# One encoder kernel: expert weights in 8 KB pieces, router weights in two steps, and another order of work at the last tile

## The chip, the cores and the metric

The kernel runs on one core of one Trainium2 chip. The metric is the device time of one launch in microseconds (us); the span of the profile, from the first to the last instruction, is some 2 us shorter. The core's engines run side by side, each with its own queue of instructions: TensorE (PE; its weight loads are a row of their own, PEld), VectorE (DVE), ScalarE (ACT), GpSimd (POOL) and SyncE (SP), which here only issues transfers. Engines wait for one another on semaphores.

## What is computed

Two encoder layers on 1024 tokens of width 1024, all in float32. Layer 0 mixes tokens by neighbourhood attention, layer 1 by a chunked two-way mLSTM scan, both beside attention to a memory. After each mixer stand an output projection, a layer norm, a router and a mixture of 16 experts:

```python
x = layer_norm(ALPHA * x + mixed @ w_out[i], ln_g[i, 0], ln_b[i, 0])
x = layer_norm(ALPHA * x + moe(x, router_w, router_b, exp_w_gate[i], exp_w_up[i], exp_w_down[i]),
               ln_g[i, 1], ln_b[i, 1])
# in moe: two experts of one group per token, and for each expert on its rows
hb = silu(xb @ w_gate[e]) * (xb @ w_up[e])
return hb @ w_down[e]
```

`w_gate` and `w_up` are 1024 x 512, `w_down` is 512 x 1024, for each of 16 experts and both layers.

## The kernel before

**Products.** A float32 product is made of three `fp32r` matmuls: both operands are split into a high part (a cast on ScalarE, `w_hi`) and the remainder (a subtraction on VectorE, `w_lo`), and `mm3` (L105 to L107) adds high x high, high x low and low x high. In the trace's names the moving operand comes first, the stationary one second: `dense<-w_hi,yh` moves 512 columns of weights past 128 loaded columns of `yh`.

**Weights** come through a `WeightStream`: `load` issues transfers on SyncE's queue into raw buffers, `split` takes the next one and splits it (L77 on ScalarE, L78 on VectorE or on an engine that is passed), `pieces` does it in halves (L92, L93) that the caller places between other work, `next` hands over a split piece. A piece of expert weights is 1 MB: 4 blocks of 128 rows x 512 columns. Row `k*128 + p` of the matrix lies on partition `p`, so a partition's 8 KB come as four runs of 2 KB.

**Tail of a layer** (`out_proj`, L1843). Eight tiles of 128 tokens: `products` of the mixer's output with `w_out` in two halves of 512 columns, `sums` (the residual, and the norm's statistics), `turn` (the transposes of the sums, L1485), `logits` (L1491), `route` (a chain of small VectorE steps to L1559, begun by `begin` and run by `choose` with other work put between its steps), `ranks` (two matmuls that count tokens ahead of each one for its expert, L1573), `entries`, and `scatter` (token lists written to memory by GpSimd). A table `mid` puts such steps behind the k-th group of matmuls in a tile's first products; the order in which the code is written sets the rest, since each engine runs its instructions in the order of the program. Behind the last tile, expert 0's tokens are found from `first_sums` and `first_list` without the list in memory, its rows are gathered (`x`, 128 rows; `xb`, 64 rows), transposed (L2039 and L2089) and multiplied by the four pieces of its gate and up weights (`chunk(0)` to `chunk(3)`). `route_order` (from L1654) sorts the experts by their counts; the order sets which weights SyncE loads next. SyncE is held until `xb` has landed (`hold`).

**Experts** (`moe`). The experts run in the order of their counts; a wide one (up to 192 rows, 8 of them) and a narrow one (128 rows) in turn. For each: gather its rows (GpSimd), transpose them (L2170, and L2176 for the last 64), gate and up products into `dense` banks of PSUM (4), then, one expert later, transpose the hidden rows (L2255, L2262) and multiply by the two down pieces into `rlg` banks (2): per 512 output columns 12 matmuls for 128 rows (`pa`) and then, for a wide expert, 8 for its last 64 (`pb`, L2298, L2299). `evac` (L2289) scales a bank into `ya` on ScalarE; GpSimd adds the rows to the result in memory. `ahead` keeps up to three pieces split in advance; `flush` runs the evictions that are due.

**Between the layers**, `moe_norm` reads the eight tiles of the result (`z`), normalises them and hands them to layer 1's input products (`xp`, L831: transposes of normalised rows; L812, L817: splits of the weight pieces). A planner, `Plan`, sets the order from each step's engine, cost and due time. The weight stream there has two raw buffers, so the third piece can be loaded once the first is split.

**Router weights** (`router_weights`, L1420) are made once, in layer 0's attention: products and sums over rows (L1439, L1440), a matmul with ones (L1444), and what follows from it.

## Time and profile before

| | us |
|---|---|
| three runs, median (lowest to highest) | 2055.79 (2053.3 to 2058.6) |
| the profiled execution | 2056.02, span 2054.0 |
| TensorE busy | 1863.0 (91%) |
| VectorE busy | 1401.3 (68%) |
| ScalarE busy | 1080.4 (53%) |
| GpSimd busy | 457.1 (22%) |
| layer 0's tail | about 470 to 610 |
| experts of layer 0 | about 610 to 998 |
| layer 0 to layer 1, first matmul of layer 1's input | 1032.69 |
| layer 1's tail | about 1463 to 1617 |
| experts of layer 1 | about 1617 to 2010 |

A row of a timeline has the start, the duration, the engine, the line of the kernel, the operation, what it writes and reads, its shape, how many were put together (x4), and in brackets how long the engine was idle before it and what ended that. A row of the waits has the waiting engine, tile and line, what it waited for, and then the total in us, how often, and the longest. TensorE's matmuls overlap, so the distance from one start to the next tells the pace, not the duration.

### The profile page before, as it was taken

What the parts mean: (1) busy time and instruction counts of PE and PEld (TensorE: products, weight loads), DVE (VectorE), ACT (ScalarE), POOL (GpSimd) and SP (SyncE); (2) the same over time, 40 slices, a digit from 0 to 9 for tenths busy, and PEclk for the clock granted to TensorE, in tenths of its full rate; (3) what the DMA queues carried; (4) which work ended last, traced back from release to release, by engine and by line L of the source; (5) the groups of instructions that cost most, each with busy time, mean ns of one, the idle gap of its engine ahead of it and who ended that gap; (6) DMA issues with size and microseconds to landing.
All of it is one profiled execution on the core that took longest, in us unless ns stands there. A gap on an engine that the chain in (4) does not pass through costs nothing. (4 is left out here: it accounts for less than half of the span.)

```text
span 2054.0 us, 27927 instructions
## 1 busy us (share of the span) xinstructions
PE 1863.0 (91%) x9860; PEld 1552.1 (76%) x9860; DVE 1401.3 (68%) x2717; ACT 1080.4 (53%) x1772; POOL 457.1 (22%) x386
## 2 busy tenths in 40 slices
PE   7999999998979999999599899998798799999991
PEld 6788888877757877777398778887687587777771
DVE  5466656677767877777576554269878687777775
ACT  4465555662236666666454555444422465666663
POOL 1132222201221222222210000065422121222211
PEclk9999999999979999999799999999899899999996
DMA  5452321135538899999632222111664789999995
GB/s 186 118 134 61 68 56 39 53 121 169 189 130 293 286 297 306 311 309 305 196 128 70 63 82 75 62 32 49 212 207 150 230 267 291 297 309 306 298 286 185
DMA packets 252978, 371.19 MB, mean 181 GB/s; under 512 B 47820, under 2 KB 120868, under 8 KB 252836
## 3 DMA queue, kind: packets, MB, share of 16 engines
q1 hardware_dynamic: 237460, 320.00, 47.5%
q0 software_dynamic: 15376, 49.38, 9.5%
q8 instruction: 79, 1.29, 0.3%
q14 instruction: 63, 0.52, 0.1%
HBM read 300.43 MB, written 65.76 MB: 178 GB/s over the span
## 5 line engine op out<-in xcount | busy, mean ns | idle before, releaser
L78 DVE TENSOR_TENSOR w_lo<-w_raw,w_hi 128x2048 fp32r<-128x2048 f32 (+1 forms) x222 | 470.4, 2126 | 191.9 <-ACT w_hi L77 188.7
L77 ACT CAST w_hi<-w_raw 128x2048 fp32r<-128x2048 f32 (+1 forms) x224 | 396.9, 1780 | 62.9 <-DMA w_raw<-in_exp_w_gate_dram 47.2
L105 PE MATMUL dense<-xT_h,w_hi 128*128 128x512 f32 (+1 forms) x544 | 226.3, 416 | 0.9 <-ACT xT_h L192 0.9
L107 PE MATMUL dense<-xT_h,w_lo 128*128 128x512 f32 (+1 forms) x544 | 208.4, 383 | 1.7 <-DVE w_lo L78 1.7
L106 PE MATMUL dense<-xT_l,w_hi 128*128 128x512 f32 (+1 forms) x544 | 208.1, 383 | 1.0 <-DVE xT_l L193 1.0
L105 PE MATMUL dense<-w_hi,xah 128*128 128x512 f32 x480 | 195.9, 408 | 0.0
L107 PE MATMUL dense<-w_hi,xal 128*128 128x512 f32 x480 | 188.3, 392 | 0.0
L106 PE MATMUL dense<-w_lo,xah 128*128 128x512 f32 x480 | 187.9, 391 | 0.0
L2291 POOL DMA_INDIRECT accd<-ya,la x30 | 80.2, 2675 | 431.1 <-ACT ya L2289 419.6
L105 PE MATMUL dense<-w_hi,yh 128*128 128x512 f32 x288 | 127.6, 443 | 10.7 <-ACT yh L1868 10.6
L106 PE MATMUL dense<-w_lo,yh 128*128 128x512 f32 x288 | 119.9, 416 | 7.6 <-DVE w_lo L93 7.6
L342 ACT ACTIVATE att_p<-att_p,att_st 128x352 f32<-128x352 f32 (+1 forms) x96 | 57.9, 604 | 128.4 <-DVE att_st L340 126.2
L584 POOL TENSOR_TENSOR bias<-bias_raw,masks 128x352 f32<-128x352 f32 (+1 forms) x96 | 85.2, 893 | 163.6 <-DVE att_st L350 145.9
L107 PEld LDWEIGHTS dense<-xT_h,w_lo 128*128 128x128 f32 x544 | 103.6, 191 | 23.2 <-DVE w_lo L78 2.6
L107 PE MATMUL dense<-w_hi,yl 128*128 128x512 f32 x288 | 120.1, 417 | 0.2 <-DVE yl L1801 0.2
L351 DVE TENSOR_SCALAR att_p<-att_p,att_st 128x256 f32<-128x256 f32 (+2 forms) x160 | 112.4, 702 | 5.7
L106 PEld LDWEIGHTS dense<-xT_l,w_hi 128*128 128x128 f32 x544 | 104.6, 192 | 8.3 <-DVE xT_l L193 1.4
L105 PEld LDWEIGHTS dense<-xT_h,w_hi 128*128 128x128 f32 x544 | 104.4, 192 | 8.2 <-ACT xT_h L192 1.0
L105 PE MATMUL rlg<-w_hi,hah 128*128 128x512 f32 x256 | 103.9, 406 | 2.7 <-ACT hah L192 2.7
L107 PEld LDWEIGHTS dense<-w_hi,xal 128*128 128x128 f32 x480 | 90.1, 188 | 20.2
L107 PE MATMUL rlg<-w_hi,hal 128*128 128x512 f32 x256 | 101.4, 396 | 3.5 <-DVE hal L193 3.5
L2215 PE MATMUL dense<-w_hi,xbc 128*128 128x512 f32 x256 | 100.8, 394 | 3.8 <-DVE xbc L193 3.8
(448 smaller groups left out, 4308.9 us busy)
## 6 DMA issues: line engine op xcount, KB each, us to landing
w_raw<-in_exp_w_gate_dram SPq DMA_DIRECT2D x64, 1024.0 KB
w_raw<-in_exp_w_up_dram SPq DMA_DIRECT2D x64, 1024.0 KB
w_raw<-in_exp_w_down_dram SPq DMA_DIRECT2D x64, 1024.0 KB
w_raw<-in_na_w_in_dram SPq DMA_DIRECT2D x20, 512.0 KB
w_raw<-in_w_out_dram SPq DMA_DIRECT2D x8, 1024.0 KB
x1d<-z SPq DMA_DIRECT2D x16, 512.0 KB
accd<-za SPq DMA_DIRECT2D x16, 512.0 KB
z<-accd SPq DMA_DIRECT2D x16, 512.0 KB
```

Source lines behind the costliest of these rows:

```text
L77: self.nc.scalar.copy(h[:, :n], t[:, :n])
L78: (eng or self.nc.vector).tensor_tensor(l[:, :n], t[:, :n], h[:, :n].bitcast(F), op=OP.subtract)
L105: nc.tensor.matmul(out, lhsT=a[0], rhs=b[0], start=first, stop=False)
L106: nc.tensor.matmul(out, lhsT=a[0], rhs=b[1], start=False, stop=False)
L107: nc.tensor.matmul(out, lhsT=a[1], rhs=b[0], start=False, stop=last)
L342: nc.scalar.activation(self.p, self.p, AF.Exp, bias=st[:, 0:1], scale=-1.0, accum_out=st[:, 1:2])
L351: nc.vector.tensor_scalar(self.p, self.p, st[:, 2:3], None, op0=OP.mult)
L584: nc.gpsimd.tensor_tensor(b[:, :nr], rev[:, w0:w0 + nr, u0:u0 + 32], nb.masks[:, half * 3 + kind].rearrange("p (a b) -> p a b", b=32)[:, :nr],
L2215: nc.tensor.matmul(pb, lhsT=c[:, kk], rhs=w[0][:, k], start=kk == 0, stop=False)
L2291: nc.gpsimd.indirect_dma_start(out=accd[layer], out_offset=bass.IndirectOffsetOnAxis(ap=la[:, 0:1], axis=0), in_=ya, in_offset=None, compu ...
```

## The change

The parts, in the order of the program:

1. `router_weights` is a generator: its first part runs behind head pair 2, the matmul with ones and the rest behind head pair 3.
2. Layer 1's tail no longer splits a piece on GpSimd at the end of the scan.
3. In a tile, `ranks(t - 2)` stands behind group 6 of the first products, not group 1; in the last tile `ranks(5)` is part of the step behind group 3.
4. Behind the last tile: expert 0's rows are transposed within that tile's second products; the transposes of the last sums and `ranks(6)` go into `chunk(0)`; `chunk(1)` and most of `chunk(2)` come before `ranks(7)`; the counts are summed before the list of expert 0's last rows, and `route_order` comes before the last tile's entries and scatters. A sixth piece is loaded earlier.
5. Expert weights are laid out with row `p*8 + k` (gate, up) or `p*4 + k` (down) on partition `p`, so that a piece is one run of 8 KB per partition; a down piece holds two k for all 1024 columns. To match, the transposes of token and hidden rows take every 8th or every 4th column (`every`).
6. The down products of both column halves run side by side in two `rlg` banks, and those of a wide expert's last 64 rows go to two `dense` banks.
7. Between the layers SyncE issues the four weight pieces and the two norm rows before the loads of `z`.

```diff
                 if i == 2:
-                    router_weights(nb.pool)
+                    router = router_weights(nb.pool)
+                    next(router)
                 if i == 3:
+                    next(router)
                     layer1_consts()
...
             tl.ws.load(3)
-            tl.ws.split(nc.gpsimd)
             tl.advance()
...
-                mid = {1: [lambda: ranks(t - 2)], 2: [lambda: turn(t - 1, 0)], 4: [lambda: turn(t - 1, 1)],
-                       7: [lambda: logits(t - 1)]}
+                mid = {2: [lambda: turn(t - 1, 0)], 4: [lambda: turn(t - 1, 1)], 7: [lambda: logits(t - 1)]}
...
                     def filled():
+                        ranks(5)
                         p = count_sums(n)
...
+                else:
+                    mid[6] = [lambda: ranks(t - 2)]
...
-            products(7, 1, {1: [lambda: first_sums(chosen, 1, rows[1], True, False)], 6: [lambda: turn(7, 0)]})
+            def turn_x(q):
+                p = bank("rtr", 2)
+                for k in range(4):
+                    nc.tensor.transpose(p[:, k * 128:(k + 1) * 128], every(x, 8, 4 * q + k), ident)
...
+            products(7, 1, {1: [lambda: first_sums(chosen, 1, rows[1], True, False)], 2: [lambda: turn(7, 0)],
+                            5: [lambda: turn_x(0)], 6: [lambda: turn_x(1)]})
             store(6)
             sums(7, 1)
...
-            turn(7, 1)
             ws.load(ws.raw_bufs)
...
             fill = norm(7)
-            chunk(0)
+            chunk(0, {0: [lambda: ranks(6)], 1: [lambda: turn(7, 1)]})
             logits(7)
-            ranks(6)
             run(ws.pieces())
-            ws.load(2, nc.scalar)
-            run(fill[:2])
+            more = entries(6)
+            run(more[:1])
             begin(7)
-            run(fill[2:])
+            run(fill)
             store(7)
-            more = ws.pieces()
-            choose(7, entries(6) + [lambda: chosen.extend(first_select(sel, [6]))] + more)
+            ws.load(ws.raw_bufs)
+            more += [lambda: chosen.extend(first_select(sel, [6]))] + ws.pieces()
+            choose(7, more)
+            n = counts(rpool)
             scatter(6, 0)
             scatter(6, 1)
             chunk(1)
-            ranks(7)
+            chunk(2, {2: [lambda: ranks(7)]})
+            p = count_sums(n)
             fill = entries(7)
...
+            route_order(rpool, p)
+            run(ws.pieces())
+            ws.load(1)
             run(fill)
             scatter(7, 0)
             scatter(7, 1)
-            chunk(2)
-            route_order(rpool)
-            run(ws.pieces())
-            ws.load(1)
             chunk(3)
...
-                return v.rearrange("o (k p) c -> p (o k) c", p=128)[:, k0:k0 + nk, c0:c0 + ncol]
+                return v.rearrange("o (p k) c -> p (o k) c", p=128)[:, k0:k0 + nk]
...
-            ws.add(chunk(wd, i, 0, 4, 0, 512), (4, 512))
-            ws.add(chunk(wd, i, 0, 4, 512, 512), (4, 512))
+            ws.add(chunk(wd, i, 0, 2), (2, 1024))
+            ws.add(chunk(wd, i, 2, 2), (2, 1024))
...
+    def every(x, n, k):
+
+        return x.rearrange("t (p k) -> t k p", k=n)[:, k]
...
-                        nc.tensor.transpose(p[:, k * 128:(k + 1) * 128], xa[:, (4 * q + k) * 128:(4 * q + k + 1) * 128], ident)
+                        nc.tensor.transpose(p[:, k * 128:(k + 1) * 128], every(xa, 8, 4 * q + k), ident)
...
-                for n in range(2):
+                pa = [bank("rlg", 2), bank("rlg", 2)]
+                for c in range(2):
                     w = ws.next()
                     ws2.append(w)
-                    pa = bank("rlg", 2)
-                    for k in range(4):
-                        mm3(nc, pa, [th[:, k], tl[:, k]], [w[0][:, k], w[1][:, k]], k == 0, k == 3)
-                    if n:
-                        flush()
+                    for k in range(2):
+                        for n in range(2):
+                            mm3(nc, pa[n], [th[:, 2 * c + k], tl[:, 2 * c + k]], [x[:, k, n * 512:n * 512 + 512] for x in w],
+                                c + k == 0, c == 1 and k == 1)
                     ahead()
                     flush()
...
-                for n in range(2 if hb is not None else 0):
-                    w = ws2[n]
-                    pb = bank("rlg", 2)
...
+                pb = [bank("dense", 4), bank("dense", 4)]
+                for c in range(2):
+                    w = ws2[c]
+                    for k in range(2):
+                        for n in range(2):
+                            for m in range(2):
+                                nc.tensor.matmul(pb[n], lhsT=tc_[:, 2 * c + k], rhs=w[m][:, k, n * 512:n * 512 + 512],
+                                                 start=c + k + m == 0, stop=c == 1 and k + m == 2)
...
-        add_load(0)
+
+        for f in extra[:2]:
+            f()
         add_row("ln_g")
-        add_load(1)
         add_row("ln_b")
-        add_load(2)
-        for t in range(3, nbuf):
-            if extra:
-                extra.pop(0)()
+        for f in extra[2:]:
+            f()
+        sums_there = plan.op([], ("d", 0.0, lambda: None), lag=0.0 if rows else 9.0)
+        for t in range(nbuf):
             add_load(t)
```

**TensorE behind the last products, layer 0's tail, before.** `L1485` and `L2039` are transposes (of the sums, and of expert 0's rows), the `dense` rows from `yh` are products.

```order
L107 MATMUL dense<-w_hi,yl 128x512
L2039 MATMUL rtr<-ident,z 128x128 x8
L1485 MATMUL rtr<-ident,z 128x128 x4
L105 MATMUL dense<-w_hi,yh 128x512
L106 MATMUL dense<-w_lo,yh 128x512
L107 MATMUL dense<-w_hi,yl 128x512
```

**The same place now**, first within the last products (`L2041` are the transposes of expert 0's rows):

```order
L2041 MATMUL rtr<-ident,z 128x128 x4
L105 MATMUL dense<-w_hi,yh 128x512
L106 MATMUL dense<-w_lo,yh 128x512
L107 MATMUL dense<-w_hi,yl 128x512
L2041 MATMUL rtr<-ident,z 128x128 x4
L105 MATMUL dense<-w_hi,yh 128x512
```

and then where `chunk(0)` has begun (`L1576`, `L1577` are the ranks, `L1488` the transposes of the sums):

```order
L1576 LDWEIGHTS tri
L1576 MATMUL rlg<-rt,tri 128x16
L1577 LDWEIGHTS onesb
L1577 MATMUL rlg<-rt,onesb 128x16
L105 MATMUL dense<-w_hi,yh 128x512
L106 MATMUL dense<-w_lo,yh 128x512
L107 MATMUL dense<-w_hi,yl 128x512
L1488 MATMUL rtr<-ident,z 128x128 x4
```

The eight transposes of expert 0's rows moved from behind the products into them, and those of the last sums from ahead of the first chunk into it; `ranks(6)` came in from behind the logits.

**TensorE in expert 0's down projection, before** (the last group of `pa` and the first rows of `pb`):

```order
L106 MATMUL rlg<-w_lo,hah 128x512
L107 MATMUL rlg<-w_hi,hal 128x512
L2170 MATMUL rtr<-ident,xa 128x128 x4
L2298 MATMUL rlg<-w_hi,hbc 128x512
L2299 MATMUL rlg<-w_lo,hbc 128x512
```

**Now:**

```order
L106 MATMUL rlg<-w_lo,hah 128x512
L107 MATMUL rlg<-w_hi,hal 128x512
L2183 MATMUL rtr<-ident,xa 128x128 x4
L2315 MATMUL dense<-w_hi,hbc 128x512
L2315 MATMUL dense<-w_lo,hbc 128x512
```

The products of the last 64 rows moved from `rlg` to `dense`; the products of `pa` alternate between two `rlg` banks, which the rows don't tell.

**SyncE's queue between the layers, before:**

```order
L2407 DMA z<-accd_73 128x1024
L243 DMA ln_g<-in_ln_g_dram 128x1024
L2407 DMA z<-accd_73 128x1024
L243 DMA ln_b<-in_ln_b_dram 128x1024
L2407 DMA z<-accd_73 128x1024
L58 DMA w_raw<-in_ml_w_in_dram 128x8x128
L2407 DMA z<-accd_73 128x1024
L58 DMA w_raw<-in_ml_w_in_dram 128x8x128
L2407 DMA z<-accd_73 128x1024
L2407 DMA z<-accd_73 128x1024
L58 DMA w_raw<-in_ml_w_in_dram 128x8x128
```

**Now:**

```order
L58 DMA w_raw<-in_ml_w_in_dram 128x8x128 x2
L243 DMA ln_g<-in_ln_g_dram 128x1024
L243 DMA ln_b<-in_ln_b_dram 128x1024
L58 DMA w_raw<-in_ml_w_in_dram 128x8x128 x2
L2424 DMA z<-accd_73 128x1024
```

All four weight pieces and both rows now stand ahead of the first `z` load; before, that load stood ahead of all of them and the pieces between the loads.

More of the change, by code (lines that the diff above doesn't have):

```diff
@@ L1442, in router_weights @@
         nc.gpsimd.memset(one, 1.0)
+        yield
         p = bank("att_t", 2)
@@ L2031, in out_proj, with chunk @@
             choose(6, fill)
-            products(7, 1, {1: [lambda: first_sums(chosen, 1, rows[1], True, False)], 6: [lambda: turn(7, 0)]})
+            xh, xl = [epool.tile([128, 8, 128], R, name=n, tag=n, bufs=2) for n in ("yh", "yl")]
+            def turn_x(q):
+                p = bank("rtr", 2)
+                for k in range(4):
+                    nc.tensor.transpose(p[:, k * 128:(k + 1) * 128], every(x, 8, 4 * q + k), ident)
+                p = p.rearrange("p (k t) -> p k t", k=4)
+                split_from_psum(xh[:, 4 * q:4 * q + 4], xl[:, 4 * q:4 * q + 4], p)
+            products(7, 1, {1: [lambda: first_sums(chosen, 1, rows[1], True, False)], 2: [lambda: turn(7, 0)],
+                            5: [lambda: turn_x(0)], 6: [lambda: turn_x(1)]})
             store(6)
             sums(7, 1)
-            xh, xl = [epool.tile([128, 8, 128], R, name=n, tag=n, bufs=2) for n in ("yh", "yl")]
-            for q in range(2):
-                p = bank("rtr", 2)
-                for k in range(4):
-                    nc.tensor.transpose(p[:, k * 128:(k + 1) * 128], x[:, (4 * q + k) * 128:(4 * q + k + 1) * 128], ident)
-                p = p.rearrange("p (k t) -> p k t", k=4)
-                split_from_psum(xh[:, 4 * q:4 * q + 4], xl[:, 4 * q:4 * q + 4], p)
-            turn(7, 1)
             ws.load(ws.raw_bufs)
             e.w, e.p = [], []
-            def chunk(j):
+            def chunk(j, after={}):
                 if j % 2 == 0:
@@ L2088, in out_proj @@
             for k in range(8):
-                nc.tensor.transpose(p[:, k * 64:(k + 1) * 64], xb[:, k * 128:(k + 1) * 128], ident[:64, :64])
+                nc.tensor.transpose(p[:, k * 64:(k + 1) * 64], every(xb, 8, k), ident[:64, :64])
             split_from_psum(e.c[:, :, 0:64], e.c[:, :, 64:128], p.rearrange("p (k t) -> p k t", k=8))
@@ L2175, in rest @@
                     for k in range(8):
-                        nc.tensor.transpose(p[:, k * 64:(k + 1) * 64], xb[:, k * 128:(k + 1) * 128], ident[:64, :64])
+                        nc.tensor.transpose(p[:, k * 64:(k + 1) * 64], every(xb, 8, k), ident[:64, :64])
                     split_from_psum(c[:, :, 0:64], c[:, :, 64:128], p.rearrange("p (k t) -> p k t", k=8))
@@ L2254, in full @@
                     for k in range(4):
-                        nc.tensor.transpose(p[:, k * 128:(k + 1) * 128], ha[:, k * 128:(k + 1) * 128], ident)
+                        nc.tensor.transpose(p[:, k * 128:(k + 1) * 128], every(ha, 4, k), ident)
                     split_from_psum(th, tl, p.rearrange("p (k t) -> p k t", k=4))
@@ L2261, in rest @@
                     for k in range(4):
-                        nc.tensor.transpose(p[:, k * 64:(k + 1) * 64], hb[:, k * 128:(k + 1) * 128], ident[:64, :64])
+                        nc.tensor.transpose(p[:, k * 64:(k + 1) * 64], every(hb, 4, k), ident[:64, :64])
                     split_from_psum(tc_[:, :, 0:64], tc_[:, :, 64:128], p[:, :256].rearrange("p (k t) -> p k t", k=4))
@@ L2286, in down, with evac @@
                         fill.pop(0)()
[L2288 to L2299 removed]
+                def evac(n):
+                    nc.scalar.mul(ya[:, n * 512:n * 512 + 512], pa[n], la[:, 1:2].bitcast(F))
+                    if n == 1:
+                        nc.gpsimd.indirect_dma_start(out=accd[layer], out_offset=bass.IndirectOffsetOnAxis(ap=la[:, 0:1], axis=0),
+                                                     in_=ya, in_offset=None, compute_op=OP.add)
+                late.extend([lambda: evac(0), lambda: evac(1)])
+                if hb is None:
+                    return
+                pb = [bank("dense", 4), bank("dense", 4)]
[6 more added lines that the diff above has]
+                                                 start=c + k + m == 0, stop=c == 1 and k + m == 2)
                     flush()
@@ L2411, in add_load @@
         def add_load(t):
-            loads.append(plan.op(ends[t - nbuf] if t >= nbuf else [], ("s", 1.5, lambda: load(t)), lag=2.0))
+            loads.append(plan.op(ends[t - nbuf] if t >= nbuf else [sums_there], ("s", 1.5, lambda: load(t)), lag=2.0))
         def add_row(key):
```

42 lines of the change are left out of this document (16 added, 26 removed).

## The prediction

> **What bounds the kernel now.** I read the page's busy line first, then the windows by stage, then TensorE's waits, and last the timelines of the places that the change touches. From the page, busy time of each engine:
>
> ```profile
> PE 1863.0 (91%) x9860; PEld 1552.1 (76%) x9860; DVE 1401.3 (68%) x2717; ACT 1080.4 (53%) x1772; POOL 457.1 (22%) x386
> ```
>
> TensorE is busy 1863.0 of 2054.0 us, so the time is TensorE's work, the gaps in it, and the extra cost of matmuls that run at a lower granted clock behind a gap. The windows show where the gaps lie (PE busy, then PEld, DVE, ACT, POOL, granted clock, DMA share, GB/s); they are tail 0, the experts of layer 0, tail 1 and the experts of layer 1:
>
> ```profile
> 470.00:620.00 150.00, 126.09 (x628) 102.36 (x626) 110.98 (x465) 42.54 (x56) 27.76 (x28) 0.91 0.52 172
> 620.00:990.00 370.00, 362.32 (x1691) 290.89 (x1692) 283.78 (x244) 240.61 (x230) 86.24 (x42) 1.00 0.92 297
> 1463.00:1625.00 162.00, 144.25 (x733) 117.23 (x734) 119.67 (x473) 47.12 (x61) 32.61 (x34) 0.94 0.56 184
> 1650.00:2010.00 360.00, 348.19 (x1618) 279.19 (x1617) 271.42 (x230) 228.78 (x219) 85.22 (x41) 0.99 0.90 289
> ```
>
> Among the experts TensorE is idle 7.7 us of 370 and 11.8 of 360, at full clock; the tails lose 23.9 and 17.8. So what makes weights arrive or be split faster is worth nothing by itself among the experts, and what lengthens TensorE's work there is paid in full. TensorE's waits name the gaps (us in total, times, longest):
>
> ```profile
> PE rlg L1573 <- DVE rt L1559: 21.2, 6, 5.7
> PE xp L831 <- DVE ln_mv L2456: 18.7, 1, 18.7
> PE rlg L2298 <- ACT ya L2289: 17.6, 22, 4.4
> PE dense L105 <- ACT yh L1868: 10.6, 1, 10.6
> PE xp L831 <- DVE z L2466: 10.1, 2, 7.4
> PE dense L106 <- DVE w_lo L93: 7.6, 2, 3.8
> PE att_t L1444 <- DVE rred L1440: 3.9, 1, 3.9
> ```
>
> Every edit is costed by what it does to one of these rows.
>
> **Down projection, banks.** The 17.6 us are TensorE waiting for one of two `rlg` banks. One place of layer 0, ScalarE and then TensorE:
>
> ```profile
> 717.75 1.91 ACT L77 CAST w_hi<-w_raw 128x2048 fp32r<-128x2048 f32 x1 [4.43 <-DMA w_raw<-in_exp_w_gate_dram]
> 720.51 0.70 ACT L2289 ACTIVATE ya<-rlg,la 128x512 f32<-128x512 f32 x1
> 721.26 0.80 PE L2298 MATMUL rlg<-w_hi,hbc 128*128 128x512 f32 x1 [2.21 <-ACT ya L2289]
> ```
>
> The eviction that frees the bank stands in ScalarE's queue behind a cast that waits for a weight piece. The change gives the second product `dense` banks. A wide expert takes four of these, the narrow one after it two, and the two that come next are the wide one's up-projection banks, read out a whole expert earlier. The late cast stays, but nothing on TensorE waits behind it: next in line is the `rlg` pair, wanted again only one expert later. I take 15 of the 17.6 us; bounds 8 (some of the waits go over to w_lo, since the split pieces sit behind the same cast) and 18.
>
> **The weight layout.** Pieces of 8 KB per partition in place of four rows of 2 KB move the same bytes; by the windows no gap of size is a weight's, so I cost the transfer itself at nothing. Its cover is the three pieces split ahead. What it adds is on TensorE: the transposes now load a stationary operand whose columns lie 32 bytes apart (16 for the hidden rows). Their groups (ns min/median/max):
>
> ```profile
> L2170 PEld LDWEIGHTS rtr<-ident,xa x240: 137/140/146, 625.8 to 1977.5; 128*128 128x128 f32 x120
> L2170 PE MATMUL rtr<-ident,xa x240: 270/272/273, 626.0 to 1977.6; 128*128 128x128 f32 x120
> L2255 PE MATMUL rtr<-ident,ha x128: 270/272/328, 613.7 to 2006.6; 128*128 128x128 f32 x128
> L2176 PE MATMUL rtr<-ident,xb x112: 221/223/273, 630.7 to 1930.5; 64*128 64x64 f32 x112
> L2262 PE MATMUL rtr<-ident,hb x64: 221/223/273, 622.8 to 1971.1; 64*128 64x64 f32 x64
> ```
>
> That is 240 + 128 + 112 + 64 = 544, and 32 more in the two tails: 576 loads of 128 columns. The trace holds no strided load on TensorE. The nearest rows are VectorE's: 128 contiguous elements, and the same 128 read 64 bytes apart.
>
> ```profile
> L1439 DVE TENSOR_TENSOR rwg<-rw,rgbT x2: 284/288/293, 184.7 to 185.3; 128x128 f32<-128x128 f32 x2
> L1440 DVE TENSOR_REDUCE rred<-rwg x2: 366/366/367, 185.1 to 185.7; 128x16 f32<-128x128 f32 x2
> ```
>
> The difference is 0.08 us for 128 elements. Bounds: nothing, if a load of 140 ns is no slower or its growth hides under the matmul before it (loads overlap matmuls, PEld being a row of its own), and 576 x 0.08 = 46 us if TensorE's loads grow as VectorE's reads do and none hides. A gain is excluded, since the contiguous read can't be the slower one. I take 10 us, nearer the lower end: the upper row is of another engine and another operation, and the rows of TensorE itself show loads that run beside matmuls, so that the first of each group of four or eight has a 512-column matmul to hide under.
>
> The Trainium skill says (SBUF — State Buffer, Specifications; Advanced Engine Details and Errata, SBUF Cachelines) that memory lines are 16 bytes and two hits on a line are needed for full rate. By that rule every column of these loads is a line of its own and the price is the upper one; VectorE's two rows agree with it, no run here shows it for TensorE.
>
> **Router weights in two steps.** The last row of the waits, 3.9 us, goes: the matmul moves a head pair later, when the reductions are long done. The two ScalarE and two VectorE operations behind it move too, to an engine with work queued, and nothing needs them before the first tile's logits. Gain 3.5; bounds 2 and 5.
>
> **Ranks later in each tile.** Of the 21.2 us four waits lie in the tile loops and two in the tails' ends; the longest is 5.7, and one of the ends is the 4.99 below, so the loops hold 21.2 - 5.7 - 5.0 = 10.5. After the change the ranks stand five matmul groups later, behind turns that need `z` sums; those are queued on VectorE behind the same routing steps, so the turn at step 4 is late next, by less. I take a gain of 6.5; bounds 2 and 10.5.
>
> **End of the last tile, twice.** TensorE, then VectorE, in layer 0:
>
> ```profile
> 573.63 1.04 PE L2039 MATMUL rtr<-ident,z 128*128 128x128 f32 x8
> 583.45 0.48 PE L105 MATMUL dense<-w_hi,yh 128*128 128x512 f32 x1
> 586.07 0.40 PE L107 MATMUL dense<-w_hi,yl 128*128 128x512 f32 x1
> 591.46 0.17 PE L1573 MATMUL rlg<-rt,tri 128*128 128x16 bf16 x1 [4.99 <-DVE rt L1559]
> 592.80 0.80 PE L105 MATMUL dense<-w_hi,yh 128*128 128x512 f32 x1
> 597.66 0.63 PE L107 MATMUL dense<-w_hi,yl 128*128 128x512 f32 x1
> 602.45 0.79 PE L106 MATMUL dense<-w_lo,yh 128*128 128x512 f32 x1 [3.77 <-DVE w_lo L93]
> 609.96 0.50 PE L2215 MATMUL dense<-w_hi,xbc 128*128 128x512 f32 x1 [1.40 <-DVE xbc L193]
> ```
> ```profile
> 591.17 0.23 DVE L1559 SCALAR_TENSOR_TENSOR rt<-rc,rt,rt 128x16 bf16<-128x16 f32 x1
> 598.37 0.16 DVE L1662 COPY rf<-rlg 1x16 f32<-1x16 f32 x1 [4.18 <-PE rlg L1638]
> 601.18 2.35 DVE L93 TENSOR_TENSOR w_lo<-w_raw,w_hi 128x1024 fp32r<-128x1024 f32 x2
> ```
>
> Twelve matmuls take 2.6 us from start to start before the gap (583.45 to 586.07) and 4.9 behind it (592.80 to 597.66). The chain is VectorE's: the last sums, the logits, the routing that ends at 591.17, the order of the experts (598.37 to 601.18, 2.8 us, waiting 4.18 us for a count that TensorE takes behind a whole chunk), the low halves, the last chunk. The change takes the eight transposes from between the last products and the logits (1 us), puts the logits behind one chunk that already overlaps the sums (some 1.5 us), and lets the count follow the ranks at once. So the ranks come at about 591.5 - 2.5 = 589; list and order take 589 + 1.5 + 2.8, the halves 2.35: 595.7 for the last chunk, at the slow pace 4.9 more, then 609.96 - 602.45 - 4.9 = 2.6 for the transposes and their eviction: 603.2. One more microsecond for the entries that VectorE now does after the order: 604, a gain of 6, 12 for both tails. Bounds 4 and 18: the early chunks only fill the wait, and VectorE keeps its serial chain. The second scatter of the last tile leaves later, and SyncE's list load and, queued behind it, the next expert's pieces wait for it; the pieces already loaded cover that, at 0 to 3 us a tail if they don't.
>
> **Scan's end.** The group of the line (ns min/median/max), then its last step and GpSimd's split beside it:
>
> ```profile
> L1315 DVE SCALAR_TENSOR_TENSOR hs<-nm,sm,hs x32: 404/408/4717, 1396.0 to 1459.5; 128x192 f32<-128x192 f32 x32
> ...
> 1454.16 5.71 DVE L1315 SCALAR_TENSOR_TENSOR hs<-nm,sm,hs 128x192 f32<-128x192 f32 x4
> 1454.51 4.49 POOL L78 TENSOR_TENSOR w_lo<-w_raw,w_hi 128x2048 fp32r<-128x2048 f32 x1 [0.81 <-ACT w_hi L77]
> ```
>
> Four such steps take 5.71 us beside GpSimd's split; by the median of the line they take 4 x 0.408 = 1.6. The split goes, so up to 4.1 us come off the chain to the 10.6 us wait; the piece is split later on ScalarE and VectorE, ahead of the products. I take 2.8; bounds 0 and 4.1.
>
> **Layer 0 to layer 1.** VectorE, SyncE's queue and TensorE:
>
> ```profile
> 1010.62 0.69 DVE L2439 BATCH_NORM_STATS2 ln_st<-z 128x6 f32<-128x512 f32 x1 [11.28 <-DMA z<-accd]
> 1015.70 1.28 DVE L2466 SCALAR_TENSOR_TENSOR z<-z,ln_mv,ln_b 128x1024 f32<-128x1024 f32 x1 [1.98 <-DMA ln_b<-in_ln_b_dram]
> 1009.90 2.77 SPq L2407 DMA_DIRECT2D z<-accd  x1
> 1032.69 0.56 PE L105 MATMUL dense<-xT_h,w_hi 128*128 128x256 f32 x1
> ```
>
> The change issues four weight pieces and the two rows ahead of all `z` loads. The 1.98 us for ln_b go, and the splits are done in the 11.28 us in which VectorE waited, not between the normalisation's steps (four of 1.2 us). Against it, the `z` loads share the queue behind 2 MB of weights. I take 4.5 off 1032.69; bounds -2 and 9.
>
> **Sum**, on the profiled execution's 2056.02 us (the median of the runs is 2055.79, the same for this purpose): 15 + 3.5 + 6.5 + 12 + 2.8 + 4.5 = 44.3 off, 10 on: 2056 - 34.3 = 2021.7, so 2022.
>
> **Rivals.** First, the strided loads cost what VectorE's rows say: 46 us on 44.3, 2058, and slower beyond doubt where TensorE's load grows a little more than VectorE's read, say 0.1 us: 2056 - 44.3 + 58 = 2069. It decides from 44.3 / 576 = 0.077 us a transpose. For it: the row, and TensorE's full windows among the experts. Against: loads overlap. By the Trainium skill's rule above it is this one. Second, waits change places: the tails keep VectorE's chain and give 4 each, the ranks give 2, the transition nothing, the banks 8: 8 + 3.5 + 2 + 8 + 1 + 0 = 22.5, less 10, 2043. For it: VectorE's share, 110.98 of 150 us in tail 0, with a serial chain in it. Third, the edits outside the experts do what I say, but among the experts nothing is won, because the missing bank hid weights that come late anyway (DMA share 0.92): 44.3 - 15 = 29.3, less 10, 2037. For it: the cast above waited 4.43 us for a piece. Against: no wait for an expert's split piece (L78) is among TensorE's rows above.
>
> **Numbers.** Forecast 0.47, first rival 0.28, second 0.15, third 0.10. A change below 0.3% (6.2 us) can't be told from none. The likeliest case alone spans 2008 to 2036 (bounds of tails, banks and strides, not all at one end). Of the first rival a third (0.09) lies within 2050 to 2062 and two thirds (0.19) above; the other three cases, 0.72, are faster. For eight in ten: 2006 to 2062.
>
> **What would show it.** The L2298 wait row gone and no new one on `dense`: the banks. The PEld median of L2170's transposes at 140 ns and eight of them still in 1.04 us: no price of the stride; above 200 ns, the first rival. First `xbc` product about 6 us earlier than before against the start of its tail: the ends. No L1444 wait; L1315 at 1.6 us for four; the two `xp` rows at 25 us or less together (now 28.8). The forecast falls if transposes cost over 0.08 us more, or if SyncE's list load holds expert 1's pieces.

## The result

| | median us | ratio to the kernel before (95% interval) |
|---|---|---|
| before | 2055.57 | 1 |
| changed | 2022.92 (2020.07 to 2025.61) | 0.983 (0.981 to 0.986) |

The forecast was 2022, and the gain is 32.6 us. That the number came out this near is luck: the experiments give the new banks of the down projection 26 us where 15 were forecast, and the ends of the last tiles some 2 where 12 were, and the two errors met. The page of the changed kernel, busy time of each engine, and then TensorE's waits in it (us in all, times, longest):

```profile
PE 1868.1 (92%) x9860; PEld 1565.4 (77%) x9860; DVE 1396.6 (69%) x2720; ACT 1081.5 (53%) x1772; POOL 464.2 (23%) x385
```
```profile
PE xp L832 <- DVE ln_mv L2472: 22.6, 1, 22.6
PE dense L106 <- DVE w_lo L93: 10.0, 4, 4.1
...
PE dense L105 <- ACT yh L1870: 6.3, 1, 6.3
PE dense L105 <- ACT w_hi L92: 6.0, 2, 3.0
PE rtr L1488 <- DVE z L1897: 5.8, 2, 4.5
PE xp L832 <- DVE xT_l L844: 4.9, 3, 2.2
...
PE rlg L105 <- ACT ya L2302: 2.5, 2, 1.3
```

The `rlg` wait of 17.6 us, the ranks' 21.2 and the router's 3.9 have no row any more. In their place stand small waits: a chunk of expert 0 for its weights' high half (6.0), a turn for its sums (5.8). The windows among the experts (PE, PEld, DVE, ACT, POOL, clock, DMA share, GB/s; layer 0, layer 1) are nearly full:

```profile
608.00:978.00 370.00, 367.55 (x1710) 301.11 (x1709) 285.46 (x247) 242.32 (x233) 93.22 (x43) 1.00 0.91 300
1620.00:1980.00 360.00, 357.56 (x1660) 293.17 (x1659) 276.82 (x238) 234.76 (x224) 89.11 (x42) 1.00 0.91 295
```

TensorE's idle time there fell from 7.7 and 11.8 us to 2.5 and 2.4. Its busy time rose by 5.1 us all the same: something on it became dearer.

**Stages.** All kernels below were profiled once; the table gives stage lengths in us between the same TensorE instructions in each: the first output product of a tail, expert 0's first `xbc` product, the last `hal` product of the experts, the last 256-column product of layer 1's input with `w_hi`. An edit that touches one stage is read there, and the other stages show how far two profiles of the same work differ: up to 4 us in the tails and among the experts, where matmuls at half the clock come and go (the same kernel took 389.1 and 385.0 us for the experts of layer 1), up to 3.4 in the first stage, and 1 to 2 elsewhere.

| kernel | up to tail 0 | tail 0 | experts 0 | between layers | layer 1 | tail 1 | experts 1 |
|---|---|---|---|---|---|---|---|
| before | 425.3 | 184.7 | 388.1 | 80.1 | 385.7 | 153.7 | 395.7 |
| changed | 422.8 | 175.4 | 383.0 | 79.1 | 379.1 | 155.8 | 389.1 |
| changed, again | 422.5 | 178.1 | 382.3 | 79.5 | 379.4 | 152.2 | 385.0 |
| b_banks | 428.4 | 184.0 | 379.2 | 78.9 | 385.2 | 153.5 | 378.4 |
| b_layout | 428.8 | 184.4 | 385.5 | 81.0 | 384.9 | 155.4 | 386.1 |
| a_8k_contig | 423.7 | 181.0 | 378.8 | 79.4 | 379.8 | 152.0 | 383.0 |
| a_contig | 422.6 | 177.5 | 380.1 | 79.0 | 378.9 | 155.4 | 383.9 |
| a_pairs | 422.7 | 181.3 | 383.1 | 79.2 | 379.5 | 155.0 | 385.8 |
| a_z_first | 421.6 | 176.1 | 382.5 | 78.9 | 379.2 | 156.0 | 385.0 |
| a_norm_old | 422.5 | 175.1 | 382.5 | 80.1 | 380.0 | 151.0 | 387.5 |
| a_ranks_old | 423.1 | 183.7 | 382.5 | 79.4 | 379.7 | 155.3 | 385.0 |
| a_scan_old | 422.7 | 181.3 | 382.3 | 79.5 | 383.4 | 151.6 | 386.5 |
| a_norm2 | 425.0 | 177.4 | 386.4 | 78.4 | 380.9 | 151.1 | 384.9 |
| best | 424.5 | 176.6 | 380.8 | 78.6 | 379.5 | 151.3 | 384.0 |

One stretch repeats far better: from expert 0's last `hal` product to that of the expert before the last, summed over both layers. The seven kernels that have the changed kernel's banks, layout and transposes all take 716.9 to 717.0 us there. The others take 733.8 (before), 707.7 (b_banks), 725.0 (b_layout), 706.5 (a_8k_contig), 707.7 (a_contig), 719.2 (a_pairs) and 708.2 (best). Below this is called the inner stretch.

### The profile page after: what moved, and what is told of

Same layout as the page of the kernel before. It is cut to its first block, busy times and chain, and to the rows that moved or that the text cites. A ratio compares the mean times of both kernels' runs of the same rounds, so it can differ in the third digit from the quotient of the medians.

```text
span 2023.7 us, 27949 instructions
## 1 busy us (share of the span) xinstructions
PE 1868.1 (92%) x9860; PEld 1565.4 (77%) x9860; DVE 1396.6 (69%) x2720; ACT 1081.5 (53%) x1772; POOL 464.2 (23%) x385
## 5 line engine op out<-in xcount | busy, mean ns | idle before, releaser
L2304 POOL DMA_INDIRECT accd<-ya,la x30 | 74.3, 2478 | 403.5 <-ACT ya L2302 392.3
L105 PEld LDWEIGHTS dense<-w_hi,xah 128*128 128x128 f32 x480 | 90.7, 189 | 17.3
```

What stands on the lines that cost most here:

```text
L105: nc.tensor.matmul(out, lhsT=a[0], rhs=b[0], start=first, stop=False)
L2304: nc.gpsimd.indirect_dma_start(out=accd[layer], out_offset=bass.IndirectOffsetOnAxis(ap=la[:, 0:1], axis=0), in_=ya, in_offset=None, compu ...
```

## The experiments

**The changed kernel again.**

> The changed kernel once more, as the measure for the three that run beside it, and a second profile of every stage. All theories: 0.983 of the kernel before, with stages that agree with the first profile within 1 us where no slow matmuls lie, and within some 4 us in the tails, where the phase of the slow matmuls differs from run to run.

It took 0.983 (0.980 to 0.986) of the kernel before on this chip, where that kernel took 2061.8 us; so what follows compares ratios and stages.

### What the stride costs, and from which stride on

Contiguous transposes with the 8 KB pieces kept; the expert products then pair rows that don't belong together, and only the time is of use:

```diff
     def every(x, n, k):
-        return x.rearrange("t (p k) -> t k p", k=n)[:, k]
+        return x.rearrange("t (k p) -> t k p", k=n)[:, k]
```

> The changed kernel with the 8 KB pieces kept, but every transpose of token and hidden rows reading 128 neighbouring columns again, as before the change. The rows of the weights and the columns of the tokens then don't match, so the expert products are of wrong pairs (their number, sizes and order are unchanged; only values differ). Theory 1, the stride costs TensorE only where the transpose moves 64 columns: in the changed kernel the eight transposes of 64 rows took 1.09 us instead of 0.71 (14 times) and the four of 64 hidden rows 0.70 instead of 0.46 (16 times), those of 128 rows 0.60 as before; 14 x 0.38 + 16 x 0.24 + 2 x 0.2 = 9.6 us, and about 1.3 for the 32 groups of hidden rows (0.64 against 0.60): 11 us less than the changed kernel's 2022.9, so 2012. Rival, the longer loads hide even there, behind matmuls that follow: 2021 to 2023.

0.977 (0.974 to 0.980) of the kernel before. The experts' stages are 4.1 and 6.2 us shorter than in the first profile of the changed kernel, 3.5 and 2.1 than in the second. The transposes of token and hidden rows, each group measured from its first start to the start of what follows, and summed over both layers, take 58.6 and 58.3 us in the two profiles of the changed kernel, 48.2 here and 48.0 before the change: the stride costs 10.2 us, and 10.4 by the inner stretch. Theory 1 holds. The groups of the changed kernel (ns min/median/max; token rows, hidden rows, the last 64 token rows, and their hidden rows), to be held against medians of 140, 140, 139 and 139 ns before:

```profile
L2183 PEld LDWEIGHTS rtr<-ident,xa x240: 186/189/194, 614.6 to 1947.8; 128*128 128x128 f32 x120
L2268 PEld LDWEIGHTS rtr<-ident,ha x128: 195/208/221, 603.3 to 1975.5; 128*128 128x128 f32 x128
L2189 PEld LDWEIGHTS rtr<-ident,xb x112: 182/203/206, 619.5 to 1902.8; 64*128 64x128 f32 x112
L2275 PEld LDWEIGHTS rtr<-ident,hb x64: 192/216/220, 611.4 to 1941.2; 64*128 64x128 f32 x64
```

And one group of four transposes of 128 rows and one of eight of 64 in the changed kernel, then the eight before the change:

```profile
614.84 0.60 PE L2183 MATMUL rtr<-ident,xa 128*128 128x128 f32 x4
...
619.52 1.09 PE L2189 MATMUL rtr<-ident,xb 64*128 64x64 f32 x8
```
```profile
630.71 0.71 PE L2176 MATMUL rtr<-ident,xb 64*128 64x64 f32 x8
```

All strided loads grew, by 49 to 77 ns. The four that move 128 columns each still take 0.60 us: the load hides. The eight that move 64 take 0.38 us more, three quarters of the 8 x 0.064 us by which their loads grew. So the price lies on the 112 + 64 + 16 transposes of 64 rows: 14 x 0.38 + 16 x 0.24 + 2 x 0.18 = 9.5 us, and a little on the hidden rows.

A layout with two neighbouring columns of 4 bytes in every 16-byte line:

```diff
...
-                return v.rearrange("o (p k) c -> p (o k) c", p=128)[:, k0:k0 + nk]
+                return v.rearrange("o (a p b) c -> p (o a) (b c)", p=128, b=2)[:, k0 // 2:(k0 + nk) // 2]
...
     def every(x, n, k):
-        return x.rearrange("t (p k) -> t k p", k=n)[:, k]
+        return x.rearrange("t (a p b) -> t a b p", a=n // 2, b=2)[:, k // 2, k % 2]
```

> The changed kernel with a third layout: row a*256 + p*2 + b on partition p, so that a weight piece comes in runs of 4 KB (gate, up) or 8 KB (down) per partition and the transposes read columns 8 bytes apart instead of 32 or 16. Theory, a load is dear when each column lies in a 16-byte line of its own (this is the rule of the Trainium skill, SBUF - State Buffer, Specifications: two hits per line for full rate): two columns per line load as fast as contiguous ones, PEld 140 ns, the stages of the experts 4 and 6 us shorter as with contiguous transposes, 0.977 to 0.979 of the kernel before. Rival, any stride costs: PEld about 190 ns, eight transposes of 64 rows in 1.09 us, 0.983.

0.983 (0.981 to 0.986), and no shorter stage. The loads at 8 bytes' distance:

```profile
L2183 PEld LDWEIGHTS rtr<-ident,xa x240: 195/204/212, 620.1 to 1952.7; 128*128 128x128 f32 x120
L2189 PEld LDWEIGHTS rtr<-ident,xb x112: 192/213/220, 625.0 to 1907.5; 64*128 64x128 f32 x112
```

They are as dear as at 16 bytes and dearer than at 32. The rule of the Trainium skill (SBUF — State Buffer, Specifications) that two hits on a line are enough doesn't hold for these loads: at none of the three distances does the median come near the 140 ns of neighbouring columns.

### Pieces and banks: one wait, removed twice

Old rows of the weights in the changed kernel (and contiguous transposes to match):

```diff
-                return v.rearrange("o (p k) c -> p (o k) c", p=128)[:, k0:k0 + nk]
+                return v.rearrange("o (k p) c -> p (o k) c", p=128)[:, k0:k0 + nk]
```

> The changed kernel with the rows of the expert weights laid out as before the change (row k*128 + p on partition p, runs of 2 KB, and of 4 KB for the down pieces) and contiguous transposes; all else of the change is kept. Theory 1, the 8 KB runs are worth nothing by themselves (the DMA share among the experts was 0.92 at 297 GB/s before and 0.91 at 300 after): 2012, as the kernel with 8 KB runs and contiguous transposes. Rival, the long runs keep the weights on time now that TensorE has no idle time left among the experts: a wait for split weights or for a weight transfer appears on TensorE there, and the time is 2018 to 2030.

0.979 (0.976 to 0.982). With the new banks in place the 8 KB runs are worth 1.2 + 1.0 us (the experts' stages against a_8k_contig), 1.2 in the inner stretch, so next to nothing, as theory 1 had it. The new banks alone, on the kernel before; the edit is the `down` of the diff above, with pieces `chunk(wd, i, 0, 2, 0, 1024)` and `chunk(wd, i, 2, 2, 0, 1024)` of the old rows:

> The kernel before with the new down projection alone (two rlg banks side by side, the last 64 rows in dense banks, down pieces of two k by 1024 columns; rows laid out as before, transposes contiguous). Theory, the 17.6 us of waits for the rlg banks go and come back nowhere: stages of the experts shorter by 6.9 and 10.7 us and some slow matmuls behind the gaps (3.7) less, 2055.6 - 19 = 2037. Rival, the bank hid a late weight piece, so a third to all of the wait turns up at the next matmul that needs split weights: 2042 to 2055.

0.987 (0.984 to 0.990). The experts' stages are 8.9 and 17.3 us shorter, and the inner stretch is 26.1: 26 us where 15 were forecast, with 18 as the upper bound. The new layout and strided transposes alone, on the kernel before:

```diff
-                return v.rearrange("o (k p) c -> p (o k) c", p=128)[:, k0:k0 + nk, c0:c0 + ncol]
+                return v.rearrange("o (p k) c -> p (o k) c", p=128)[:, k0:k0 + nk, c0:c0 + ncol]
...
-                        nc.tensor.transpose(p[:, k * 128:(k + 1) * 128], xa[:, (4 * q + k) * 128:(4 * q + k + 1) * 128], ident)
+                        nc.tensor.transpose(p[:, k * 128:(k + 1) * 128], every(xa, 8, 4 * q + k), ident)
```

> The kernel before with the new rows of the expert weights and the strided transposes alone (gate and up pieces in 8 KB runs, down pieces still 512 columns in 2 KB runs). Theory, this part of the change is a loss by itself: transposes 10 us dearer, the longer runs worth 2, so 8 us more, 1.004 of the kernel before. Rival, some of the dearer transposes fall into TensorE's waits for the rlg banks, 17.6 us in all, and cost nothing there: 2 to 5 us more, not to be told from none.

0.994 (0.992 to 0.996): faster, where both theories said slower. The experts' stages are 2.5 and 9.6 us shorter, the inner stretch 8.8, in spite of transposes that take 10 us more. If that is paid in full here, the longer runs are worth some 19 to 22 us; whether a part of it hides in waits, as the rival had it, was not tried. What they act on is ScalarE's wait for gate pieces. The rows of the kernel before, of b_banks and of b_layout, in this order:

```profile
ACT w_hi L77 <- DMA w_raw<-in_exp_w_gate_dram: 47.2, 18, 5.7
```
```profile
ACT w_hi L77 <- DMA w_raw<-in_exp_w_gate_dram: 45.4, 21, 5.1
```
```profile
ACT w_hi L77 <- DMA w_raw<-in_exp_w_gate_dram: 25.8, 11, 3.8
PE rlg L2302 <- ACT ya L2293: 4.0, 11, 1.2
```

The new banks leave ScalarE's wait at 45 us, and TensorE no longer minds. The new layout halves ScalarE's wait, and TensorE's 17.6 us for the bank shrink to 4.0. One place in two kernels, SyncE's issue of the second gate piece and ScalarE's cast of it, before and after the change:

```profile
706.46 0.37 SPq L58 DMA_DIRECT2D w_raw<-in_exp_w_gate_dram  x1
```
```profile
695.69 0.33 SPq L58 DMA_DIRECT2D w_raw<-in_exp_w_gate_dram  x1
...
705.84 1.90 ACT L77 CAST w_hi<-w_raw 128x2048 fp32r<-128x2048 f32 x1 [2.25 <-DMA w_raw<-in_exp_w_gate_dram]
```

The cast waited until 717.75 before, 11.3 us behind the issue, and 10.2 us now. Either edit removes nearly the whole stall: TensorE's idle time in the experts' stages is 25.4 us before, 7.2 in b_banks, 6.8 in b_layout and 8.0 in the changed kernel. Together they are worth 14 us in these stages (783.8 us before, 772.1 and 767.3 in the two profiles of the changed kernel), not 26 + 12, and 16.9 in the inner stretch, not 26.1 + 8.8. So with the banks in place the layout is a loss: it brings 1.2 us and its stride costs 10.4. The DMA share and rate among the experts (0.92 at 297 GB/s, 0.91 at 300) didn't show it; the wait of the engine that uses the piece did.

### Between the layers

```diff
-        for f in extra[2:]:
-            f()
-        sums_there = plan.op([], ("d", 0.0, lambda: None), lag=0.0 if rows else 9.0)
+        sums_there = plan.op([], ("d", 0.0, lambda: None), lag=0.0 if rows else 5.0)
         for t in range(nbuf):
+            if t == 3:
+                for f in extra[2:]:
+                    f()
             add_load(t)
```

> The changed kernel, but between the layers SyncE issues the loads of the first three z tiles ahead of weight pieces 3 and 4 (pieces 1 and 2 and the rows of the norm still first). In the changed kernel the z loads were issued 9.5 us behind the last scatter's issue (992.83 after 983.36), before the change 6.1 us (1007.11 after 1000.98). Theory, the 1 MB of pieces 3 and 4, issued at 986.72, shares the DMA engines with the scatter and stands ahead of z: without it z is issued 3 us sooner and the first matmul of layer 1's input comes 3 to 5 us sooner, 2019. Rival, the splits of pieces 3 and 4 then stand between the norm's steps on VectorE again and take it back: 2022 to 2024.

No difference: 0.983, and 78.9 us in the stage against 79.1 and 79.5. GpSimd's last scatter and SyncE's first `z` loads before the change, with the change, and here:

```profile
1000.98 1.56 POOL L2291 DMA_INDIRECT accd<-ya,la  x1 [6.24 <-issue]
...
1007.11 0.35 SPq L2407 DMA_DIRECT2D z<-accd  x1
```
```profile
983.36 1.56 POOL L2304 DMA_INDIRECT accd<-ya,la  x1 [5.36 <-DVE xm L882]
...
992.83 2.72 SPq L2424 DMA_DIRECT2D z<-accd  x6
```
```profile
982.45 1.56 POOL L2304 DMA_INDIRECT accd<-ya,la  x1 [5.24 <-DVE xm L882]
...
992.11 1.29 SPq L2424 DMA_DIRECT2D z<-accd  x3
```

With pieces 3 and 4 behind `z`, the load is still issued 9.7 us behind the scatter's issue, so these pieces are not what delays it. What is left of the expectation's mechanism are the two pieces and the two rows that stand ahead of the scatter in both kernels. With the whole old order in the changed kernel (`add_load(0)`, `add_row("ln_g")`, `add_load(1)` and so on, as in the lines with a minus):

> The changed kernel with the order of transfers between the layers as before the change. The stage from the last expert's matmul to the end of layer 1's first input products was 80.1 us before (78.9 in the kernel with the new banks alone) and 78.5 to 79.4 in the kernels with the new order. Theory, the new order is worth nothing: 78.5 to 80 here, since the two pieces and the two rows that now go ahead share the DMA engines with the last scatter, whose z load comes 9.5 us behind it instead of 6.1. Rival, it is worth the 4.5 us forecast: 83 or more.

0.984 (0.982 to 0.985), and 80.1 us: the new order is worth about 1 us of the 4.5 forecast, no more than two profiles differ by.

```profile
982.67 1.56 POOL L2304 DMA_INDIRECT accd<-ya,la  x1 [5.53 <-issue]
...
988.82 0.34 SPq L2424 DMA_DIRECT2D z<-accd  x1
```

Here the load follows the scatter's issue by 6.2 us again. So the transfers that the change puts ahead of the scatter delay its end by some 3.4 us; which of the four does it was not tried.

### Ranks, norm steps, GpSimd's split

```diff
-                mid = {2: [lambda: turn(t - 1, 0)], 4: [lambda: turn(t - 1, 1)], 7: [lambda: logits(t - 1)]}
+                mid = {1: [lambda: ranks(t - 2)], 2: [lambda: turn(t - 1, 0)], 4: [lambda: turn(t - 1, 1)], 7: [lambda: logits(t - 1)]}
...
-                        ranks(5)
...
-                else:
-                    mid[6] = [lambda: ranks(t - 2)]
```

> The changed kernel with the ranks behind the first matmul group of a tile again, as before the change. Theory, moving them was worth less than the 10.5 us of its waits, because the turn at step 4 then waits for sums that stand behind the same routing steps on VectorE (4.5 us in tile 2 of layer 0): the first seven tiles were 135.2 and 138.0 us in layer 0 in two kernels with the old place and 132.3 to 135.4 with the new, so 2 to 4 us longer here, and 1 to 3 in layer 1; 0.2% in all. Rival, it is worth the 6.5 us forecast: 0.3 to 0.4%.

0.986 (0.984 to 0.987). From a tail's first product to the logits of tile 6 it is 137.8 and 112.3 us, against 134.0 and 109.6, the means of the kernels with the new place (a_scan_old left out of the second): 6.5 us, as forecast. Among these kernels alone the two spread by 3 us each, 132.2 to 135.4 and 108.7 to 111.5; and the three kernels made from the one before, 137.1 and 108.6 in the mean, against 134.0 and, for layer 1, a_scan_old's 107.3, give 4.4. The waits are back, at the size of 10.5 that was worked out for them, and less than their whole is gained since the turns wait instead:

```profile
PE rlg L1576 <- DVE rt L1562: 11.0, 4, 3.7
```
```profile
483.01 1.02 PE L1488 MATMUL rtr<-ident,z 128*128 128x128 f32 x4 [4.49 <-DVE z L1897]
```

The second fence is the changed kernel. Now the norm steps:

```diff
             run(more[:1])
+            run(fill[:2])
             begin(7)
-            run(fill)
+            run(fill[2:])
```

> The changed kernel with the first two of the last tile's four norm steps put ahead of the routing steps again, where VectorE waits for the logits, as before the change. Theory, the tails' ends gained little because the change put all four steps into VectorE's routing chain: from the logits to the last ranks it was 9.8 us before and 12.8 after (layer 0: 581.70 to 591.46, 571.26 to 584.09). Two steps are 1.4 us, so the ranks and the first xbc product come 1.4 us sooner after the logits in both tails, 0.1% of the time. Rival, TensorE's chunks set the place of the ranks, or VectorE is busy with low halves before the logits anyway: less than 0.5 us.

The theory fell. From the logits to the ranks it is 575.80 to 588.61, 12.8 us as in the changed kernel. VectorE starts the routing steps 1.3 us later instead, as the rival had it: the time from the last sums on VectorE to the end of the routing is 14.18 us in both. The ratio of 0.982 (0.980 to 0.984) is not to be told from 0.983. And the split on GpSimd:

```diff
             tl.ws.load(3)
+            tl.ws.split(nc.gpsimd)
             tl.advance()
```

> The changed kernel with GpSimd's split of one piece at the scan's end back again. Theory, the missing split is worth the 4.3 us between 10.6 and 6.3 of the wait ahead of layer 1's first output product, but the piece is split on VectorE among the products then and costs 1 to 3 us in that tail: here the stage of layer 1 is 4 to 6 us longer and the first seven tiles of its tail 1 to 3 us shorter, 0.1 to 0.2% slower in all. Rival, the tail doesn't care: 6 us slower in all, 0.3%.

0.984 (0.982 to 0.987). Layer 1 is 3.8 us longer than the mean of the others (383.4 against 379.6), the way to tile 6's logits in its tail 2.3 shorter (107.3 against 109.6), and TensorE's wait is back:

```profile
PE dense L105 <- ACT yh L1871: 10.6, 1, 10.6
```

In the changed kernel the longest single step of VectorE's line is 1.2 us, where it was 4.7:

```profile
L1316 DVE SCALAR_TENSOR_TENSOR hs<-nm,sm,hs x32: 404/411/1177, 1376.1 to 1435.0; 128x192 f32<-128x192 f32 x32
```

So the split beside it costs 3.8 us there, and more than half comes back where the piece is split later.

### The parts that pay, together

The changed kernel with contiguous transposes, the old rows of the weights (as in a_contig) and the norm steps of a_norm2:

> The changed kernel with the old rows of the expert weights and contiguous transposes (2 and 4 KB runs), and with two norm steps ahead of the routing steps in the last tile. Theory: the stride's 10 us less 2 to 3 for the shorter runs, and 2 to 3 for the two norm steps: 9 to 11 us under the changed kernel, 0.978 of the kernel before. Rival, the shorter runs bring weights late now that nothing else stalls among the experts: 0.981 to 0.983.

0.981 (0.979 to 0.983), a median of 2017.94 us beside 2060.06 for the kernel before. That is faster than the kernel before; its interval overlaps that of the changed kernel, so that it beats that one too is likely by the experts' stages (764.8 us against 772.1 and 767.3) and the inner stretch (708.2 against 717.0), and not shown by the times. The theory's 0.978 wasn't reached; late weights, the rival's reason, are not seen, since the inner stretch is within 0.5 us of a_contig's. a_contig and this kernel differ by an edit that was found to do nothing.

## Why the prediction came out right, step by step

| step | forecast us | measured us | from |
|---|---|---|---|
| banks | -15 | -26 | b_banks, inner stretch |
| 8 KB pieces | 0 | -1, with the banks in place | a_8k_contig against a_contig, inner stretch |
| strided transposes | +10 | +10 | transposes summed over both layers |
| router in two steps | -3.5 | -4.4 | first stage, mean of 3 kernels 427.5 (425.3 to 428.8), of 11 others 423.1 (421.6 to 425.0) |
| ranks later | -6.5 | -4.4 to -6.5 | a_ranks_old, and the kernels with the old place |
| ends of the last tile | -12 | -2 | from the logits of tile 6 to the end of expert 0, below |
| scan's end | -2.8 | -1.5 | a_scan_old, 3.8 less 2.3 |
| between the layers | -4.5 | -1 | a_norm_old |

The measured column adds up to -30 to -32, near the 32.6 us of the result.

**The banks: right mechanism, wrong size, and not alone.** "I take 15 of the 17.6 us" was too little, and the upper bound of 18 too: alone the edit is worth 26. TensorE's idle time among the experts fell by 18.2 us (25.4 to 7.2) and its busy time by 8.1 (758.4 to 750.4), which the wait's row doesn't hold; what the second part consists of was not taken apart.

**The pieces: wrong.** The step that failed is "by the windows no gap of size is a weight's, so I cost the transfer itself at nothing". The wait for the bank was a weight's wait: the row quoted for the banks showed the late gate piece on ScalarE, 4.43 us of it. The longer runs alone are worth some 19 to 22 us before the stride's 10. The error did no harm because both edits end the same stall: beside the new banks the pieces bring 1.2 us, so the term of nothing came out right for a wrong reason. The third rival, that late pieces would take the gain, is out: b_banks kept ScalarE's late pieces and won all the same.

**The stride: right in size, half right in its reason.** The bounds held, and the choice near the lower one did too. The reason given, a 512-column matmul to hide the first of a group, is not it: transposes of token rows that move 128 columns hide the longer load throughout, and those that move 64 hide a quarter of it. The first rival needed 0.077 us a transpose; the runs give 10 / 576 = 0.017. VectorE's rows were no measure for TensorE's loads on the path, though the load itself grew by much of their 0.08 us.

**The tails' ends: right where they were looked at, lost on both sides of it.** VectorE's last sums and the end of its routing in the changed kernel, layer 0, and TensorE's first `xbc` product:

```profile
568.64 0.68 DVE L1899 SCALAR_TENSOR_TENSOR z<-xres,dense 128x512 f32<-128x512 f32 x1
...
582.82 0.23 DVE L1562 SCALAR_TENSOR_TENSOR rt<-rc,rt,rt 128x16 bf16<-128x16 f32 x1
```
```profile
598.16 0.50 PE L2228 MATMUL dense<-w_hi,xbc 128*128 128x512 f32 x1 [1.40 <-DVE xbc L193]
```

That is 29.5 us from sums to product. It is 34.1 to 36.1 in the three kernels with the old end (six tails) and 28.7 to 29.9 in those with the new one: 5.2 us a tail, where 6 were worked out. Ahead of the sums the same stretch, from the logits of tile 6, grew from 11.1 to 13.4 us to 12.5 to 16.5: the transposes that moved there, and the slow matmuls of the last section. This is why tail 1 shows no gain in the first profile. Behind the product, up to expert 0's last `hal` product, layer 0 takes 16.7 us in the mean with the old end and 16.9 with the new, but layer 1 takes 17.1 and 20.0; why is not worked out. Over the whole stretch, from the logits of tile 6 to expert 0's last `hal` product, layer 0 went from a mean of 64.0 us (62.3 to 65.3) to 61.2 (59.0 to 63.8), and layer 1 from 62.8 (61.7 to 64.2) to 63.7 (60.8 to 67.0). So the edit is worth some 2 us and not 12, less than its lower bound of 4. The step that failed is "a gain of 6, 12 for both tails": it followed the chain from the last sums to the `xbc` product, and left out the time that the moved transposes and slow matmuls take ahead of the sums, and what follows behind the product.

**Between the layers: the step that failed** is "the splits are done in the 11.28 us in which VectorE waited". They were, but that wait didn't stay where it was: `z` came 9.5 us behind the scatter, not 6.1. The bound of -2 to 9 held. The sign named for it came true and misled: the `xp` row fell from 28.8 us to 22.6, but 4.9 came back as a wait of `xp` for `xT_l`.

The second rival (waits change places everywhere, 2043) fell with the banks and the ranks. Two of its parts were nearer than the forecast's, though: nothing for the transition, and little for the tails, which gave some 1 us each where it had 4.

## What to carry to other kernels

When a wait names a bank or a buffer, look at what stands ahead of the eviction in its engine's queue: if it is a late transfer, a faster transfer and a free buffer are two cures for one stall, and their gains don't add. A strided operand on TensorE is to be priced by the instruction that it loads for: here hidden where 128 columns move, mostly exposed where 64 do. A loss and a gain of one edit, here 10 us of stride against some 20 of earlier weights, are only seen apart when each half is run by itself, and the gain may be gone once another edit has ended the same stall. And a reordering is to be measured over a stretch that holds everything that it moved.

## What was not expected of the hardware

**The clock falls with hardly a gap.** Behind the logits of tile 6, TensorE's clock halved in 21 of the 28 tails profiled, though TensorE stood idle for no more than 0.6 us in the 12 us before. The changed kernel in layer 1's tail: logits with 16 columns and sums with 3, then products at half the pace, and the windows of 5 us there (PE busy, PEld, DVE, ACT, POOL, clock, DMA share, GB/s):

```profile
1549.03 1.85 PE L1494 MATMUL rlg<-rwg,x1T 128*128 128x16 f32 x16
1550.73 1.99 PE L1618 MATMUL dense<-tk,yt 128*128 128x3 f32 x12
1552.58 0.77 PE L105 MATMUL dense<-w_hi,yh 128*128 128x512 f32 x1
```
```profile
1545.00:1550.00 5.00, 4.49 (x30) 3.83 (x29) 2.88 (x24) 0.70 (x2) 1.98 (x2) 1.00 0.02 4
1550.00:1555.00 5.00, 5.00 (x26) 4.38 (x26) 2.20 (x9) 0.22 (x1) 0.89 (x1) 0.65 0.00 0
1555.00:1560.00 5.00, 5.00 (x24) 3.99 (x23) 4.65 (x24) 0.58 (x1) 1.84 (x2) 0.50 0.61 208
1560.00:1565.00 5.00, 5.00 (x24) 4.17 (x23) 1.56 (x9) 1.39 (x3) 0.00 (x0) 0.82 0.00 2
```

The granted clock is 0.50 for a window in which the row counts TensorE as busy throughout; the 0.51 us of idle time in the first window lie 3 us ahead of the logits. In a_norm2, with 0.49 us of idle time at the same place, it stays at 1.00:

```profile
1555.00:1560.00 5.00, 5.00 (x38) 4.59 (x37) 1.44 (x6) 0.58 (x1) 1.03 (x1) 1.00 0.02 3
1560.00:1565.00 5.00, 5.00 (x35) 4.08 (x35) 4.32 (x16) 0.81 (x2) 2.69 (x2) 1.00 0.15 25
```

From the logits to the last sums that takes 12.5 us there and 16.4 in the changed kernel. The clock records of the traces have the halved clock last 3.4, 6.8 or 10.2 us. That it is a matter of when the few columns fall is argued from this; the halving is why the tails' stages differ by some 4 us between profiles of one kernel. The Trainium skill (TensorE: Matmul & The Clock Gate, What's actually happening) has the clock follow activity in a window that runs free of the program, which fits the equal steps of 3.4 us; that few moving columns count as idle is read from these rows and wasn't tried by itself.

**A load at 8 bytes' distance is no cheaper than at 16 or 32**: medians of 204, 208 and 189 ns for 128 rows, and 140 side by side.
